# Two passes of 512-wide products for the last 1024 output columns of a hybrid encoder layer

## The chip, the cores and the metric

The kernel runs on one core of a Trainium2 chip. Its time is the device time of one execution in microseconds; where several executions were timed, the median is given. A profiled execution is a separate one, with a span (first to last instruction) of its own.

## What is computed

One layer of an encoder: 512 tokens of width 2048 are normalised and projected; eight attention heads and a bidirectional linear recurrence each make 1024 features per token; these 2048 mixed features are gated and projected back by `w_out`, and the residual `x` is added. The change concerns the last line alone.

```python
h = rms_norm(x, norm_w)
q, k, v, g_attn, xr, g_lru = split(h @ w_in)
...
mixed = concatenate([rms_norm(attn_out, attn_norm_w) * silu(g_attn),
                     rms_norm(lru_out, lru_norm_w) * silu(g_lru)], axis=-1)
return x + mixed @ w_out          # (512 x 2048) @ (2048 x 2048)
```

## The kernel before, in words

Everything is float32. A matrix product is made of three matmuls on numbers split in a high and a low part (high x high, high x low, low x high), each part in the type float32r. The split of a weight tile is a cast on ScalarE (the high part) and a subtraction on VectorE (the low part).

The stages run one behind the other on TensorE: the input projections (`proj_feat`, `proj_tok`, whose matmuls are on lines 145 to 147), recurrence, attention, gates, and then `outputs` (line 729). The order of TensorE's instructions is the program's own (`manual_schedule`, line 825). On the other engines a list scheduler orders them by priority; `tc.high_priority(AHEAD)` moves what prepares the weights 600 places ahead.

`outputs` works in four groups `c` of 512 output columns. Within a group the loop `i` runs over eight row pairs of `mixed`, that is 2 x 128 rows of `w_out`. `wraw` (line 189) loads a pair's 2 x 128 x 512 block of `w_out` (512 KB) on SyncE's queue, into one of three buffers.

The first six pairs are multiplied by a two-by-two block scheme with seven products instead of eight. The blocks on the weight side are 128 rows by 256 columns (`H`), those on the features' side 128 features by 256 tokens. `combine` (line 682) makes the block sums, `seven` (line 696) splits the three plain blocks and the four sums (768 + 1024 columns) into high and low parts, and `mult` (line 744) issues a product's matmuls, line 752: two blocks of 128 tokens, three terms, 256 columns each, 42 matmuls per pair. Four of the products (`P1`, `Q6`, `Q5`, `Q7`) go into shared sums in four PSUM banks of tag `pj`, the other three straight into the banks of their outputs, tag `mm`. Behind pair 5 the shared sums are combined (lines 805 to 812) into `comb` and added to `xt`, which holds `x`.

The last two pairs, 6 and 7, are split by `four` (line 704) and multiplied whole, by `whole` (line 762, matmuls on line 773): 24 matmuls of 512 columns per pair. In the last group one token block is done in halves of 256 columns, so that the final addition and store are short. At a group's end VectorE adds the banks to `xt` (line 818), and SyncE stores it (line 819).

The stationary side of these matmuls is the features' side, split and combined once and used by all four groups. `kept` (line 714) gives it its tiles, through `aside` (line 709), which makes a tile 16 floats longer and uses it from the eighth float on. The pairs 4 to 7 are prepared by `later` (line 965) and `last_gates` (line 985), a generator that `outputs` advances one step per pair in group 0. `wkept` (line 719) gives the moving side one of three sets of buffers in turn. `hring` and `aring` (lines 99 and 100) are rings that hold the recurrence's and the attention's outputs; an eight-float tile `pad` (line 102) is allocated behind them.

Of the kernel before, what the change touches and what calls it, by code (L numbers as in the profile page):

```python
# [16 lines left out]
P = 128  # L17
SEQ = 512
# [37 lines left out]
def hybrid_kernel(  # L56
# [69 lines left out]
    def ev():  # L126

        for pool, n in (("lru", 4), ("qkv", 8), ("fin", 4)):
            if pool in pools:
                return pools[pool].tile([P, SEQ], F32, tag="ev", bufs=n, name=nm("ev"))  # L130
# [58 lines left out]
    def wraw(w, r0, c0, nk=1, queue=nc.sync):  # L189

        raw = pools["wr"].tile([P, 2, SEQ], F32, tag="wr", bufs=3, name=nm("wr"))
# [486 lines left out]

    def halves(t):
# [49 lines left out]
    def outputs(work):  # L729

        for c in range(DM // SEQ):
            xt, comb = (
                pools["out"].tile([P, NT, SEQ], F32, tag=t, bufs=1, name=nm(t)) for t in ("xt", "cb")
            )
            cs = slice(c * SEQ, (c + 1) * SEQ)
            rows_ = [slice(t * P, (t + 1) * P) for t in range(NT)]
            for t in range(NT):
                nc.sync.dma_start(xt[:, t], xf[rows_[t], cs])

            acc = {k: pj().rearrange("p (s e) -> p s e", e=H) for k in (P1, Q6, Q5, Q7)}  # L740
            own = [mm() for _ in range(NT)]
            fresh = set(acc) | set(range(NT))

            def mult(k, s, ah, al, a, bh, bl, b_, last):
                ts_ = slice(s * P, (s + 1) * P)
                if k in acc:
                    dst, bank = acc[k][:, s, :], k
                else:
                    bank = s if k == Q4 else 2 + s
                    dst = own[bank][:, H:] if k in (P2, Q4) else own[bank][:, :H]  # L750
                for lh, rh in ((ah, bh), (ah, bl), (al, bh)):
                    nc.tensor.matmul(  # L752
                        dst, lh[:, a, ts_], rh[:, b_, :], start=bank in fresh,
                        stop=last and s == 1 and rh is bh and lh is al, skip_group_check=True,
                    )
                    fresh.discard(bank)


            end = c == DM // SEQ - 1
            lasts = [pj()[:, :H], own[1][:, H:]] if end else []  # L760

            def whole(t, ah, al, bh, bl, last):

                ts_ = slice(t % 2 * P, (t % 2 + 1) * P)
                for half in range(2 if t == 1 and end else 1):
                    for k in range(2):
                        a, w = 2 * k + t // 2, slice(2 * k, 2 * k + 2)
                        dst = own[t].rearrange("p (j e) -> p j e", e=H)
                        if t == 1 and end:
                            dst, w = lasts[half], 2 * k + half  # L770
                        for j, (lh, rh) in enumerate(((ah, bh), (ah, bl), (al, bh))):
                            new = t == 1 and end and half == 0 and k == 0 and j == 0 and not last
                            nc.tensor.matmul(  # L773
                                dst, lh[:, a, ts_], rh[:, w], start=new,
                                stop=last and k == 1 and j == 2, skip_group_check=True,
                            )

            for i, (r0, A) in enumerate(mixed):
                with tc.high_priority(AHEAD):
                    (raw,) = wraw(w_out, r0, c * SEQ)  # L780
                    if i < 6:
                        bh, bl = wkept(7)
                        seven(raw, ALU.add, bh, bl)
                    else:
                        bh, bl = wkept(4)
                        four(raw, bh, bl)
                if c == 0:
                    next(work, None)
                    A = mixed[i][1]
                ah, al = A  # L790
                if i < 6:
                    for k in (P1, Q6, Q5, Q7, P2, Q3, Q4):
                        for s in range(2):
                            mult(k, s, ah, al, k[0], bh, bl, k[1], i == 5 and k in (P1, Q6, Q5, Q7))
                else:
                    for t in (2, 3, 0, 1):
                        whole(t, ah, al, bh, bl, i == 7)
                if i == 5:
# [244 lines left out]
```

## Time and profile before

| | us |
|---|---|
| median of 3 runs (lowest, highest) | 665.76 (665.64, 665.89) |
| the profiled execution | 667.75 |
| its span | 666.0 |
| output groups in the span, from and to | 497.7 to 662.3 |

The views read here are the page (busy time of each engine, the chain of work that ended last, groups of instructions by line), the windows (busy time in stretches of the span), the timeline and the DMA issues. PE is TensorE's matmuls, PEld its weight loads, which overlap the matmuls, DVE VectorE, ACT ScalarE, POOL GpSimd, SP SyncE. Matmuls are pipelined: a row's mean ns is the time from a matmul's start to its end, and the next one starts before that. What a matmul costs in a stream is therefore read from a stretch of the chain divided by the number of matmuls in it.

### The profile page before, as it was taken

The page shows a single profiled execution, that of the slowest core. Times are in us where ns is not written, and L with a number is a line of the kernel's source. Part 1 is how long each engine was busy: PE and PEld are TensorE (multiplying, and loading weights), DVE is VectorE, ACT ScalarE, POOL GpSimd, SP SyncE. Part 2 cuts the span into 40 slices and gives each one's busy share as a digit, 9 for nine tenths or more (in the row PEclk, how much of TensorE's full clock was granted, in tenths as well). Part 3 has the DMA queues.
Part 4 walks back from the last instruction along what each step waited for, and adds up shares of the span by engine and source line. Part 5 has one row for each costly group of instructions (what it writes and reads, how often), then busy time and mean ns, then how long its engine had stood idle before and what let it go on. Part 6 is the DMA issues. An engine that isn't in the chain of part 4 may idle for free.

```text
span 666.0 us, 9502 instructions
## 1 busy us (share of the span) xinstructions
PE 660.9 (99%) x3599; PEld 570.4 (86%) x3599; DVE 488.8 (73%) x820; ACT 330.4 (50%) x580; POOL 58.8 (9%) x79
## 2 busy tenths in 40 slices
PE   9999999999999999999999999999999999999997
PEld 7888888888888888888888888888889999899996
DVE  4878788977688864656955577449989994967944
ACT  3533798589766416444734465345435333332320
POOL 0000000000022303011222212110000000000000
PEclk9999999999999999999999999999999999999999
DMA  8843252322334312322111221223335373462711
GB/s 287 284 118 105 64 165 65 95 63 75 85 126 127 101 57 63 95 64 63 53 44 63 64 64 36 68 87 95 94 105 181 113 216 115 141 197 76 252 32 63
DMA packets 43773, 71.06 MB, mean 107 GB/s; under 512 B 2776, under 2 KB 13136, under 8 KB 43728
## 3 DMA queue, kind: packets, MB, share of 16 engines
q1 hardware_dynamic: 43408, 69.93, 34.3%
q10 hardware_dynamic: 320, 0.53, 0.3%
q8 instruction: 28, 0.46, 0.3%
q14 instruction: 17, 0.14, 0.1%
HBM read 66.25 MB, written 4.19 MB: 106 GB/s over the span
## 4 chain that ended last, share of the span: by engine, by line
PE 97%; DVE 1%; DMA 1%; issue 0%; ACT 0%; ACTq 0%; DVEq 0%
PE pj L145 19%; PE pj L147 19%; PE pj L146 19%; PE pj L752 10%; PE mm L752 8%; PE mm L773 6%; PE mm L145 3%; PE mm L147 3%; PE mm L146 3%; PE mm L592 2%; PE pj L298 1%; PE mm L232 1%; DMA wr<-in_w_in_dram 1%; PE mm L535 1%; DVE k L412 0%; DVE wl L207 0%
## 5 line engine op out<-in xcount | busy, mean ns | idle before, releaser
L145 PE MATMUL pj<-x,wh 128*128 128x512 f32 x376 | 149.2, 397 | 0.0
L147 PE MATMUL pj<-x,wl 128*128 128x512 f32 x376 | 147.0, 391 | 0.0
L146 PE MATMUL pj<-x,wh 128*128 128x512 f32 x376 | 146.4, 389 | 0.0
L207 DVE TENSOR_TENSOR wl<-wr,wh 128x512 fp32r<-128x512 f32 x144 | 100.8, 722 | 29.7 <-ACT wh L206 29.6
L206 ACT CAST wh<-wr 128x512 fp32r<-128x512 f32 x143 | 85.6, 618 | 68.6 <-PE pj L147 25.7
L147 PEld LDWEIGHTS pj<-x,wl 128*128 128x128 f32 x376 | 70.6, 188 | 15.3
L145 PEld LDWEIGHTS pj<-x,wh 128*128 128x128 f32 x376 | 70.6, 188 | 13.7 <-DVE ev L377 0.5
L146 PEld LDWEIGHTS pj<-x,wh 128*128 128x128 f32 x376 | 70.7, 188 | 13.4
L145 PE MATMUL pj<-wh,x 128*128 128x512 f32 x192 | 74.9, 390 | 0.0
L147 PE MATMUL pj<-wh,x 128*128 128x512 f32 x192 | 74.8, 389 | 0.0
L146 PE MATMUL pj<-wl,x 128*128 128x512 f32 x192 | 74.7, 389 | 0.0
L752 PE MATMUL pj<-wl,mh 128*128 128x256 f32 x192 | 54.0, 281 | 0.0
L752 PE MATMUL pj<-wh,ml 128*128 128x256 f32 x192 | 54.0, 281 | 0.0
L752 PE MATMUL pj<-wh,mh 128*128 128x256 f32 x192 | 53.9, 281 | 0.0
L701 ACT CAST wh<-wr 128x768 fp32r<-128x768 f32 x24 | 20.1, 836 | 63.6 <-issue 47.1
L594 ACT CAST b<-mm 128x512 fp32r<-128x512 f32 x32 | 18.7, 586 | 61.5 <-PE mm L592 61.5
L580 DVE TENSOR_REDUCE mx<-mm 128x1 f32<-128x512 f32 x32 | 22.0, 688 | 33.0 <-PE mm L147 32.4
L146 PEld LDWEIGHTS pj<-wl,x 128*128 128x128 f32 x192 | 36.0, 188 | 7.5
L145 PEld LDWEIGHTS pj<-wh,x 128*128 128x128 f32 x192 | 36.0, 188 | 7.5
L147 PEld LDWEIGHTS pj<-wh,x 128*128 128x128 f32 x192 | 36.0, 188 | 7.5
L752 PE MATMUL mm<-wl,mh 128*128 128x256 f32 x144 | 40.5, 281 | 0.0
L752 PE MATMUL mm<-wh,ml 128*128 128x256 f32 x144 | 40.5, 281 | 0.0
(216 smaller groups left out, 1335.5 us busy)
## 6 DMA issues: line engine op xcount, KB each, us to landing
wr<-in_w_in_dram SPq DMA_DIRECT2D x71, 512.0 KB, 3.7
wr<-in_w_out_dram SPq DMA_DIRECT2D x32, 512.0 KB, 4.0
xt<-in_x_dram SPq DMA_DIRECT2D x16, 256.0 KB, 4.6
out_dram<-xt SPq DMA_DIRECT2D x15, 256.0 KB, 3.6
b<-in_x_dram SPq DMA_DIRECT2D x7, 512.0 KB, 9.2
k<-in_lru_wa_dram SPq DMA_DIRECT2D x8, 128.0 KB, 3.7
k<-in_lru_wx_dram SPq DMA_DIRECT2D x8, 128.0 KB, 3.3
b<-in_x_dram SPq DMA_DIRECT2D x2, 256.0 KB, 5.3
```

What stands on the lines that cost most here:

```text
L145: nc.tensor.matmul(acc, lh, rh, start=start, stop=False)
L146: nc.tensor.matmul(acc, lh, rl, start=False, stop=False)
L147: nc.tensor.matmul(acc, ll, rh, start=False, stop=stop)
L206: copy(hi, raw[:, k, :])
L207: nc.vector.tensor_sub(lo, raw[:, k, :], f(hi))
L232: nc.tensor.transpose(pt[:, t * P : (t + 1) * P], xc[:, t, ks], ident)
L580: nc.vector.tensor_reduce(mx, sc, axis=AX.X, op=ALU.max, negate=True)
L592: nc.tensor.transpose(pt[:, s * P : (s + 1) * P], p[:, s * P : (s + 1) * P], ident)
L594: nc.scalar.copy(pth[:, :, tt], p3)
L701: nc.scalar.copy(hi[:, to], part)
L752: nc.tensor.matmul(dst, lh[:, a, ts_], rh[:, b_, :], start=bank in fresh, stop=last and s == 1 and rh is bh and lh is al, skip_group_check ...
L773: nc.tensor.matmul(dst, lh[:, a, ts_], rh[:, w], start=new, stop=last and k == 1 and j == 2, skip_group_check=True,)
```

## The change

The groups 0 and 1 stay as they were, without the special last group. The groups 2 and 3 become one group of 1024 columns, `outputs_wide`. Its blocks are 512 columns wide, and all eight pairs go by seven products. Three of the products run in a first pass over the eight pairs, four in a second, since each product's sum now takes two banks and eight are there.

- First pass: each pair's `w_out` block is read without its last quarter, two block sums are added in place, three blocks are split. The three sums (`P1`, `Q6`, `Q5`) are combined at the end of the pass into `xs`; `x` is added to `xs` by eight accumulating DMAs that GpSimd's queue issues, in place of eight loads on SyncE's.
- Second pass: each pair's block is read again, whole; two plain blocks and two sums are split, in two sets of the weight buffers. In pair 7 the order of the two sets is turned round. At the end VectorE adds or subtracts the four sums (`Q7`, `Q4`, `Q3`, `P2`) into `xs`, and SyncE stores 128 x 512 pieces, the last of them in halves.
- The raw blocks lie in the space of `aring` (two) and in that of the weight ring (one).
- Since pairs 6 and 7 now need the block sums of the features' side too, `last_sums` makes them during group 1.
- `kept` no longer goes through `aside`, and `pad` is allocated ahead of the rings instead of behind them. `wraw` takes its buffers from a ring of the same size.

```diff
-    opened("wr", "left")
+    wring = opened("wr", "left").ring(3 * 4096, name="wring")
...
+    opened("pad", "right").tile([P, 8], F32, name="pad")
     hring = opened("hq", "right").ring(8 * 2048, name="hring")
     aring = pools["hq"].ring(8 * 2048, name="aring")
-    opened("pad", "right").tile([P, 8], F32, name="pad")
...
     def kept(pool, n=7):
-        return [
-            aside(lambda *a: pool.tile(*a, tag=t, bufs=1, name=t), n)
-            for t in (nm("mh"), nm("ml"))
-        ]
+        return [pool.tile([P, n, H], F32R, tag=t, bufs=1, name=t) for t in (nm("mh"), nm("ml"))]
...
+        rings = [aring, aring, wring]
+        def raw_blocks(i, n, turn):
+            raw = rings[turn % 3].tile([P, 4, SEQ], F32, name=nm("wr"))
+            r0 = mixed[i][0]
+            for k in range(2):
+                w = slice(cs[0].start, cs[0].start + min(2, n - 2 * k) * SEQ)
+                nc.sync.dma_start(
+                    raw[:, 2 * k : min(n, 2 * k + 2)].rearrange("p j e -> p (j e)"),
+                    w_out[r0 + k * P : r0 + (k + 1) * P, w],
+                )
+            return raw
+        def parts(blocks, n):
+            hi, lo = (t.rearrange("p n e -> p (n e)") for t in wkept(7))
+            hi, lo = (t[:, : n * SEQ].rearrange("p (n e) -> p n e", e=SEQ) for t in (hi, lo))
+            nc.scalar.copy(hi, blocks)
+            nc.vector.tensor_sub(lo, blocks, f(hi))
+            return hi, lo
+        def product(k, dst, i, b, n):
+            ah, al = part(i, k[0])
+            bh, bl = (t[:, n] for t in b)
+            for s in range(2):
+                ts_ = slice(s * P, (s + 1) * P)
+                for j, (lh, rh) in enumerate(((ah, bh), (ah, bl), (al, bh))):
+                    nc.tensor.matmul(
+                        dst[s], lh[:, ts_], rh, start=i == 0 and j == 0, stop=i == 7 and j == 2
+                    )
+        p1, q6, q5 = [pj(), pj()], [pj(), pj()], [mm(), mm()]
+        for i in range(8):
+            with tc.high_priority(AHEAD):
+                raw = raw_blocks(i, 3, i)
+                nc.vector.tensor_add(raw[:, 0], raw[:, 0], raw[:, 1])
+                nc.vector.tensor_add(raw[:, 2], raw[:, 2], raw[:, 0])
+                b = parts(raw[:, 0:3], 3)
+            for k, dst, n in ((P1, p1, 1), (Q6, q6, 2), (Q5, q5, 0)):
+                product(k, dst, i, b, n)
+        with tc.high_priority(AHEAD):
+            for s in range(2):
+                nc.scalar.copy(xs[1][:, 2 + s], p1[s])
+            for s in range(2):
+                nc.vector.tensor_sub(xs[1][:, s], xs[1][:, 2 + s], q6[s])
+            for s in range(2):
+                nc.vector.tensor_sub(xs[0][:, 2 + s], q5[s], xs[1][:, s])
+                nc.scalar.copy(xs[0][:, s], xs[0][:, 2 + s])
+            for t in range(NT):
+                for j in (0, 1):
+                    nc.gpsimd.dma_start(xs[j][:, t], xf[tokens[t], cs[j]], accum_op=ALU.add)
+        q3, p2, q7, q4 = [mm(), mm()], [pj(), pj()], [pj(), pj()], [mm(), mm()]
+        for i in range(8):
+            with tc.high_priority(AHEAD):
+                raw = raw_blocks(i, 4, 8 + i)
+                bs = [((Q3, q3, 0), (P2, p2, 1), parts(raw[:, 2:4], 2))]
+                nc.vector.tensor_add(raw[:, 0:2], raw[:, 0:2], raw[:, 2:4])
+                nc.vector.tensor_add(raw[:, 1], raw[:, 1], raw[:, 0])
+                bs.append(((Q7, q7, 0), (Q4, q4, 1), parts(raw[:, 0:2], 2)))
+            for *ks, b in bs[::-1] if i == 7 else bs:
+                for k, dst, n in ks:
+                    product(k, dst, i, b, n)
+        with tc.high_priority(AHEAD):
+            def add(t, j, acc, op=ALU.add, leave=True, cut=1):
+                for m in range(cut):
+                    e = slice(m * SEQ // cut, (m + 1) * SEQ // cut)
+                    nc.vector.tensor_tensor(xs[j][:, t, e], xs[j][:, t, e], acc[:, e], op=op)
+                    if leave:
+                        to = slice(cs[j].start + e.start, cs[j].start + e.stop)
+                        nc.sync.dma_start(of[tokens[t], to], xs[j][:, t, e])
+            for s in range(2):
+                add(s, 0, q7[s])
+                add(s, 1, q7[s], ALU.subtract, False)
+            for s in range(2):
+                add(s, 1, q4[s])
+            for s in range(2):
+                add(2 + s, 0, q3[s])
+            for s in range(2):
+                add(2 + s, 1, p2[s], cut=1 + s)
...
+    def last_sums():
...
+        for i, (hi, lo) in zip((6, 7), places):
+            for _ in range(2):
+                yield
+            sums_of[i] = [[t[n // 2][:, n % 2] for n in range(4)] for t in (hi, lo)]
+            res = combine(halves(ap_[i - 4]), ALU.subtract)
+            for n in range(2):
+                src = res[:, 2 * n : 2 * n + 2]
+                nc.scalar.copy(hi[n], src)
+                nc.vector.tensor_sub(lo[n], src, f(hi[n]))
-    outputs(last_gates())
+    outputs(0, last_gates())
+    outputs(1, last_sums())
+    outputs_wide(2)
```

More of the change, by code (lines that the diff above doesn't have):

```diff
@@ L727, in wkept @@
         ]
[L729 to L736, printed above, removed]
-            for t in range(NT):
[L738 to L798, printed above, removed]
-                    with tc.high_priority(AHEAD):
-                        def blk(i, j):
-                            return comb[:, 2 * i : 2 * i + 2, j * H : (j + 1) * H]
-                        v2 = fin_s((P, 2, H))
-                        nc.scalar.copy(blk(1, 1), acc[P1])
-                        nc.vector.tensor_sub(v2, acc[Q6], blk(1, 1))
-                        nc.vector.tensor_add(blk(1, 0), acc[Q5], v2)
-                        nc.vector.tensor_add(blk(0, 0), acc[Q7], blk(1, 0))
-                        nc.vector.scalar_tensor_tensor(
-                            blk(0, 1), acc[Q7], -1.0, v2, op0=ALU.mult, op1=ALU.subtract
-                        )
-                        nc.vector.tensor_add(xt, xt, comb)
-            with tc.high_priority(AHEAD):
-                parts = [(t, 0, SEQ, own[t]) for t in (2, 3, 0, 1)]
-                if end:
-                    parts[3:] = [(1, j * H, (j + 1) * H, lasts[j]) for j in range(2)]
-                for t, e0, e1, src in parts:
-                    nc.vector.tensor_add(xt[:, t, e0:e1], src, xt[:, t, e0:e1])
-                    nc.sync.dma_start(
-                        of[rows_[t], cs.start + e0 : cs.start + e1], xt[:, t, e0:e1]
-                    )
```

96 lines of the change are left out of this document (92 added, 4 removed).

## The prediction, as it was made

> **What bounds the kernel now.** I read the page's parts 1 and 4 first. The second line is the chain of work that ended last, by engine.
>
> ```profile
> PE 660.9 (99%) x3599; PEld 570.4 (86%) x3599; DVE 488.8 (73%) x820; ACT 330.4 (50%) x580; POOL 58.8 (9%) x79
> PE 97%; DVE 1%; DMA 1%; issue 0%; ACT 0%; ACTq 0%; DVEq 0%
> ```
>
> The end is set by the matmul stream alone; the other engines matter only where they would make it wait. So the question is how many microseconds of matmul issue the change takes out, and whether the stream stays fed. Next the windows view, on a projection stage, the four output groups (the change replaces the third and the fourth), and the two kinds of stretch inside the third.
>
> ```profile
> 70.00:220.00 150.00, 150.00 (x663) 124.22 (x662) 122.98 (x178) 118.75 (x216) 11.54 (x15) 1.00 0.33 97
> 497.70:538.90 41.20, 41.20 (x302) 39.07 (x301) 40.07 (x56) 19.70 (x23) 0.00 (x0) 1.00 0.44 139
> 538.90:579.90 41.00, 41.00 (x302) 38.87 (x301) 30.50 (x43) 13.40 (x15) 0.00 (x0) 1.00 0.48 151
> 579.90:620.90 41.00, 41.00 (x302) 38.87 (x301) 30.41 (x42) 13.30 (x15) 0.00 (x0) 1.00 0.49 154
> 620.90:662.30 41.40, 41.39 (x313) 39.57 (x311) 23.78 (x30) 9.74 (x11) 0.00 (x0) 1.00 0.32 109
> 579.90:609.90 30.00, 30.00 (x254) 30.00 (x253) 19.54 (x28) 9.72 (x11) 0.00 (x0) 1.00 0.52 168
> 609.90:620.90 11.00, 11.00 (x49) 8.87 (x49) 10.86 (x15) 3.58 (x4) 0.00 (x0) 1.00 0.39 116
> ```
>
> The columns are the stretch, its length, then busy time of PE, PEld, DVE, ACT and POOL, the granted clock, the DMA share and GB/s. PE has no gap in any group. DVE is nearly full in the first group (40.07 of 41.2) and has 10 us or more to spare in each later one; ACT and DMA are under half. In the seven-product stretch (579.9 to 609.9) the weight loads are busy all 30.00 us; in the stretch of 512-wide matmuls behind it they are not (8.87 of 11.0). The chain in order of time gives the pace of each shape (start, length, what):
>
> ```profile
> 568.84 11.15 PE mm L773 x48
> 579.99 2.83 PE pj L752 x24
> 582.82 2.12 PE mm L752 x18
> 599.88 2.88 PE pj L752 x24
> 602.77 2.16 PE mm L752 x18
> 661.58 0.73 PE mm L773 x6
> ```
>
> A row pair by seven products costs 2.83 + 2.12 = 4.95 us for 42 matmuls of 256 columns, 118 ns each; a later one 2.88 + 2.16 = 5.04, 120 ns each. A pair computed whole costs 11.15 / 2 = 5.57 us for 24 matmuls of 512 columns, 232 ns each. The projection's 512-wide matmuls go faster: 150 us / about 661 (two of the 663 only touch the edges) is 227 ns.
>
> **The change, part by part.**
>
> *Matmuls of the last 1024 columns.* Before, from 579.99 to the end of the last piece at 661.58 + 0.73 = 662.31: 82.3 us, PE full. After: 8 pairs x 7 products x 2 token blocks x 3 terms = 336 matmuls, all 512 wide. Two savings are in this: two 256-wide matmuls (236 ns) become one 512-wide one, and the two pairs that were computed whole (8 block products) take seven. At 227 ns the 336 cost 76.3 us, at 232 they cost 78.0. So the term is -6.0 or -4.3 us. I take 227: the stationary tiles of the 232 ns matmuls are the ones that `kept` places through `aside`, eight floats in, the projection's are not placed so, and the change takes `aside` away from `kept` and puts the 32-byte pad elsewhere. That the placement is the cause of the 5 ns is my reading of the code; no row separates it, so 232 stays as the other end.
>
> The Trainium skill, page "TensorE: Matmul & The Clock Gate", section "Back-to-back issue gap", gives N / 2.4 + 2.5 ns for matmuls back to back: 109 ns at 256 and 216 at 512. By it widening saves almost nothing per column, and the term would be, as an estimate, 504 x 109.2 + 96 x 215.8 - 336 x 215.8 = -3.2 us. The trace has 118 and 227 to 232, so its fixed part per matmul is four times the page's, and the measured figures decide.
>
> *Groups one and two.* They keep 42 matmuls of 256 columns for six pairs and 24 of 512 for two, but their stationary tiles move too. If the 96 whole matmuls go from 232 to 227 ns that is -0.5 us; the other end is 0. For the 504 of 256 columns the present pairs lie between 4.95 and 5.04 us, so I take 0, with -0.5 us below. Above, the nearest rows of 512-wide matmuls on differently placed tiles are these (busy us, mean ns):
>
> ```profile
> L145 PE MATMUL mm<-kt,b 128*128 128x512 f32 x32 | 12.9, 404 | 0.0
> L147 PE MATMUL pj<-wh,x 128*128 128x512 f32 x192 | 74.8, 389 | 0.0
> ```
>
> 404 - 389 = 15 ns more for each; on 504 matmuls +7.6 us is the far end.
>
> *Splitting the weights.* Rows by form, mean ns:
>
> ```profile
> L702 DVE TENSOR_TENSOR wl<-t,wh 128x1024 fp32r<-128x1024 f32 x24 | 29.2, 1220 | 1.1 <-ACT wh L701 1.1
> L702 DVE TENSOR_TENSOR wl<-wr,wh 128x768 fp32r<-128x768 f32 x24 | 22.9, 953 | 12.5 <-ACT wh L701 12.3
> L701 ACT CAST wh<-t 128x1024 fp32r<-128x1024 f32 x24 | 25.0, 1047 | 9.5 <-DVE t L689 9.5
> L701 ACT CAST wh<-wr 128x768 fp32r<-128x768 f32 x24 | 20.1, 836 | 63.6 <-issue 47.1
> L687 DVE TENSOR_TENSOR t<-wr 128x512 f32<-128x512 f32 x24 | 16.4, 687 | 12.7 <-DMA wr<-in_w_out_dram 12.6
> L453 DVE TENSOR_TENSOR b<-b,b 128x1024 f32<-128x1024 f32 x8 | 9.6, 1213 | 0.0
> L818 DVE TENSOR_TENSOR xt<-mm,xt 128x512 f32<-128x512 f32 x15 | 10.0, 683 | 6.0 <-PE mm L773 6.0
> L812 DVE TENSOR_TENSOR xt<-xt,cb 128x2048 f32<-128x2048 f32 x4 | 9.2, 2289 | 0.1
> ```
>
> Pass one, per pair, on DVE: two 512-wide adds (2 x 0.687) and one subtraction of 1536 columns, 1.04 ns a column from the first two rows, so 1.22 + 0.53 = 1.75 us: 3.1 us beside 18 x 227 ns = 4.1 us of matmul. ACT: one cast of 1536, 0.82 ns a column, 1.5 us. Pass two: 1.21 + 0.69 + 2 x 1.22 = 4.3 us of DVE and 2.1 of ACT beside 24 x 227 = 5.45 us. Both engines fit. If DVE ran strictly in order and waited out each cast, pass one would take 4.6 us per pair, 0.5 too many; over eight pairs that is 4 us, and the three buffer sets hold two pairs (8 us) of lead. So 0, with the seams below as its price. Group two takes on `last_sums`: two times a combination (0.69 + 2 x 0.42), two casts and two subtractions of 512, about 5.8 us of DVE. Its 30.5 busy of 41.0 us holds that.
>
> *Loads.* Pass one reads three 256 KB blocks per pair in 4.1 us (192 GB/s), pass two four in 5.45 (192 GB/s). SP issues 32 loads in place of 16; raw loads wait for a ring slot, and behind them on SP stand stores and further loads that nothing needs soon. The busiest stretch of the present output part, and the landing times:
>
> ```profile
> 538.90:548.90 10.00, 10.00 (x86) 10.00 (x85) 9.50 (x16) 3.67 (x4) 0.00 (x0) 1.00 0.86 274
> wr<-in_w_out_dram SPq DMA_DIRECT2D x32, 512.0 KB, 4.0
> ```
>
> 274 GB/s at a share of 0.86 means 319 at a full share, so 192 fits, at 0.60. The first raw tiles lie in `aring`, whose head pairs are last read in `last_sums` halfway through group two; the 4 us of landing is covered.
>
> *Seams.* At the end of pass one ACT copies two banks and DVE subtracts four (0.68 each) before the new sums may take the banks. P1 and Q6 end 2.7 and 1.4 us before the pass does, and pass two starts in two free banks (Q3, 1.4 us), takes P1's next, and needs Q5's last of all, 4.1 us in. Covered on paper; DVE work queued behind these subtractions is pair two's splitting, with a pair of lead. I allow +0.5 us for all seams (0 to +2). The eight accumulating x loads sit on POOL, which is idle here (0.00 in the windows above), and are needed 40 us later.
>
> *Tail.* Now one 256-wide add follows the last matmul, and the last stores land:
>
> ```profile
> 662.33 0.42 DVE L818 TENSOR_TENSOR xt<-mm,xt 128x256 f32<-128x256 f32 x1 [0.29 <-PE mm L773]
> 663.00:664.00 1.00, 0.00 (x0) 0.00 (x0) 0.00 (x0) 0.00 (x0) 0.00 (x0) 1.00 0.93 304
> ```
>
> After, DVE has nine adds of 512 and two of 256 behind the last pair, and Q7's first block is ready 21 matmuls (4.8 us) before the last matmul ends, at E. From E - 4.8 the queue takes 9 x 0.683 + 2 x 0.42 = 7.0 us: done at E + 2.2, where it is now E + 0.44. That is +1.8 us. Stores of 2.1 MB must leave in the same 7 us, 300 GB/s, just the 304 of the last row, so +0.4 more. Tail +2.2 us (+1.5 to +3).
>
> **Sum.** -6.0 - 0.5 + 0 + 0 + 0.5 + 2.2 = -3.8 us. The profiled execution took 667.75 us around a span of 666.0; its span would become 662.2. The runs' median is 665.76, so the forecast is **662.0 us**, 0.57% faster. A difference of about 0.2% (1.3 us) is what a measurement of this kernel can tell from none.
>
> **The rivals.**
>
> *Pace.* The wide matmuls stay at 232 ns and so do the whole ones: -4.3 + 0.5 + 2.2 = -1.6, 664.2 us. For it: every 512-wide row with these tiles is at 232. Against: all other 512-wide stages are at 227. Chance 0.13.
>
> *Narrow matmuls slow down.* The 504 of groups one and two lose by their new placement. At 5 ns each +2.5 us: 664.5; from 7.5 ns (3.8 us / 504) the change is lost. For it: `aside` is used for just such tiles, and their weight loads are already busy all the time. Against: no row shows a slower 256-wide matmul. Chance 0.12.
>
> *Starved (slower than before).* The accumulating loads hold the DMA engines and pass two waits for weights. Its 8.4 MB of weights and 2.1 MB of x at 319 GB/s take 32.9 of 43.6 us, 10.7 spare; 2.1 MB plain is 6.6 us. Accumulation must read both sides, and no row shows one. It decides when it takes 2.6 times as long as a plain load; at four times pass two lacks 19.8 - 10.7 = 9.1 us, net +5.3, 671.1 us. For it: DMA is the only resource that the change loads far more (154 to over 190 GB/s). Against: the lead in the buffers. Chance 0.20. The Trainium skill, page "DMA: Bandwidth & Descriptors", section "Issuing engines are not separate DMA queues", says that transfers of all issuers run on the same 16 engines and interleave, which is this rival's premise; before has too few issues from another queue to test it.
>
> The forecast itself has 0.55. **Range** 660.0 to 668.0: below it lies a gain at 118 ns with no seam and a short tail, above it most of the starved case. Faster by over 0.2%: 0.55 + most of the pace case + a quarter of the narrow one = 0.67; within: 0.10; slower: 0.23.
>
> **What would show it.** Right: the chain gives 18 wide matmuls in 4.1 us and 24 in 5.45; 48 whole ones in 10.9; no PE gap at the pass seam; DVE ends about 2.2 us behind the last matmul. Wrong: pairs of group one above 5.04 us (narrow), wide matmuls at 232 (pace), PE waiting on DVE or DMA for weights in pass two with a DMA share near 0.9 (starved), or a tail over 3 us longer.

## The result and the profile after

The changed kernel took **670.62 us** (median of 5 runs, 668.22 to 671.05); the kernel before, on the same chip, 665.68 us (665.4 to 665.89). The ratio is 1.0067, with a 95% interval of 1.0049 to 1.0086: 0.67% slower, where 0.57% faster was forecast. The profiled execution took 671.05 us, with a span of 669.3.

The two profiled executions start their output part at different times (the first output matmul at 497.61 us before, at 495.72 after). In the other traces it lies at 495.2 to 495.6, with the old placement of the tiles (p2 below) and with the new one (p1, e1), and at 496.6 to 497.0 with a tile of 32 to 128 bytes added; and the profiled execution of before, 667.75, is itself 2 us above its median. So these 2 us are not the change's (they are there before 21 us of the trace), and the parts are compared from the first output matmul to the end of the span: 168.4 us before, 173.6 after, **+5.2 us**.

The page of the changed kernel, busy times and then the chain of work that ended last, by engine:

```profile
PE 654.9 (98%) x3323; PEld 554.2 (83%) x3323; DVE 497.5 (74%) x818; ACT 337.3 (50%) x582; POOL 66.1 (10%) x87
PE 84%; DVE 8%; DMA 6%; issue 1%; SPq 0%; ACT 0%; DVEq 0%; ACTq 0%
```

Before, 97% of the chain was PE. Now 8% of it is DVE and 6% DMA: the matmul stream waits for something. The windows view says where (stretch, length, busy time of PE, PEld, DVE, ACT and POOL, granted clock, DMA share, GB/s):

```profile
497.60:538.90 41.30, 40.80 (x297) 38.54 (x296) 41.20 (x58) 18.84 (x23) 0.00 (x0) 1.00 0.53 175
578.80:611.50 32.70, 32.70 (x146) 27.04 (x145) 22.10 (x23) 11.98 (x10) 0.00 (x0) 1.00 0.68 216
615.00:620.00 5.00, 5.00 (x23) 3.86 (x21) 2.64 (x5) 3.14 (x5) 2.27 (x3) 1.00 1.00 229
620.00:625.00 5.00, 2.74 (x12) 2.17 (x12) 5.00 (x5) 1.03 (x1) 2.56 (x3) 1.00 0.90 168
625.00:630.00 5.00, 5.00 (x23) 4.13 (x23) 0.21 (x1) 2.11 (x2) 0.86 (x2) 1.00 1.02 266
630.00:635.00 5.00, 1.75 (x8) 1.11 (x7) 3.30 (x4) 1.04 (x1) 0.87 (x1) 1.00 1.08 303
635.00:640.00 5.00, 5.00 (x17) 3.92 (x16) 3.90 (x5) 1.05 (x1) 0.00 (x0) 0.66 0.94 245
640.00:662.90 22.90, 22.90 (x102) 18.76 (x100) 16.68 (x19) 6.33 (x6) 0.00 (x0) 1.00 0.24 87
```

Pass one (second row) is full: 32.7 us for eight times 18 matmuls, 4.08 us a pair, as forecast. Pass two is not. PE is busy 2.74 of 5 us from 620 and 1.75 of 5 us from 630, and from 635 it has a mean granted clock of 0.66. In just these 25 us the DMA share is 0.90 to 1.08, so the 16 engines have no idle time left, and afterwards it is 0.24. POOL, which issues the accumulating loads, is busy in the rows from 615 to 635 and in neither row ahead of them. The first row, nearly all of it group one, is a smaller surprise: DVE is busy 41.20 of 41.30 us.

The chain of waits in order of time (start, length, what) shows what ends the longer stall (lines left out are marked by dots):

```profile
613.90 5.99 DMA wr<-in_w_out_dram
...
622.36 0.33 SPq L829
...
622.74 8.84 DMA wr<-in_w_out_dram
...
631.70 1.23 DVE wr L881
632.93 1.15 DVE wl L839
...
634.12 1.62 PE mm L848 x5
635.74 4.16 PE pj L848 x12
639.90 2.74 PE mm L848 x12
```

A block takes 5.99 us to land; only when it is split can SP issue the next one into its buffer, at 622.36, and that one lands 8.84 us after its start: a late block makes a later one late. DVE, which has waited for it, adds and splits it (2.4 us), and PE, idle since 630.7, starts at 634.1. The next 12 matmuls take 4.16 us, and the 12 behind them 2.74: half the clock for a while, then the full one. Added up from the starts of the matmuls in the trace and set against 227 ns each, pass two waits 2.4 us at 619.7 and 3.4 us at 630.5, loses 1.7 us at half clock, and some 0.3 in small waits, **7.9 us** in all.

The tail, the same windows and the DVE timeline of the changed kernel:

```profile
663.00:664.00 1.00, 0.09 (x1) 0.00 (x0) 1.00 (x3) 0.00 (x0) 0.00 (x0) 1.00 1.10 334
665.00:666.00 1.00, 0.00 (x0) 0.00 (x0) 0.00 (x0) 0.00 (x0) 0.00 (x0) 0.97 1.12 321
667.00:668.00 1.00, 0.00 (x0) 0.00 (x0) 0.00 (x0) 0.00 (x0) 0.00 (x0) 0.50 0.29 78
```
```profile
658.32 0.69 DVE L893 TENSOR_TENSOR xt<-xt,pj 128x512 f32<-128x512 f32 x1 [1.09 <-PE pj L848]
663.11 1.34 DVE L893 TENSOR_TENSOR cb<-cb,pj 128x512 f32<-128x512 f32 x3
```

The additions run from 658.32 to 664.45, 1.5 us behind the last matmul's end at 662.9; then the stores drain, at 321 to 334 GB/s up to 666 and more slowly up to 667.8. From the start of the last matmul to the end it is 6.6 us, and was 4.0: +2.6.

### The profile page after: what moved, and what is told of

Its sections match the earlier page's. It is cut to its first block, busy times and chain, and to the rows that moved or that the text cites. A ratio compares the mean times of both kernels' runs of the same rounds, so it can differ in the third digit from the quotient of the medians.

```text
span 669.3 us, 8999 instructions
## 1 busy us (share of the span) xinstructions
PE 654.9 (98%) x3323; PEld 554.2 (83%) x3323; DVE 497.5 (74%) x818; ACT 337.3 (50%) x582; POOL 66.1 (10%) x87
## 4 chain that ended last, share of the span: by engine, by line
PE 84%; DVE 8%; DMA 6%; issue 1%; SPq 0%; ACT 0%; DVEq 0%; ACTq 0%
PE pj L145 19%; PE pj L147 19%; PE pj L146 19%; DMA wr<-in_w_out_dram 5%; PE mm L145 3%; PE mm L147 3%; PE mm L146 3%; PE pj L749 3%; PE mm L749 2%; PE mm L592 2%; PE pj L848 2%; PE mm L762 2%; PE mm L848 2%; DVE wl L839 2%; DVE wl L704 1%
## 5 line engine op out<-in xcount | busy, mean ns | idle before, releaser
L838 ACT CAST wh<-wr 128x1024 fp32r<-128x1024 f32 (+1 forms) x24 | 28.6, 1196 | 58.1 <-PE mm L848 22.7
L839 DVE TENSOR_TENSOR wl<-wr,wh 128x1024 fp32r<-128x1024 f32 (+1 forms) x24 | 33.4, 1397 | 4.7 <-ACT wh L838 4.7
L585 POOL TENSOR_SCALAR k<-k,sm 128x512 f32<-128x512 f32 x32 | 24.1, 753 | 124.0 <-DVE sm L584 112.5
L595 DVE TENSOR_TENSOR b<-mm,b 128x512 fp32r<-128x512 f32 x32 | 22.1, 689 | 12.1 <-ACT b L594 12.1
L749 PE MATMUL pj<-wh,ml 128*128 128x256 f32 x96 | 27.2, 283 | 0.0
L749 PE MATMUL pj<-wl,mh 128*128 128x256 f32 x96 | 27.2, 283 | 0.0
```

Source lines behind the costliest of these rows:

```text
L585: nc.gpsimd.tensor_scalar(p, p, sm, 0.0, op0=ALU.mult, op1=ALU.add)
L595: nc.vector.tensor_sub(ptl[:, :, tt], p3, f(pth[:, :, tt]))
L749: nc.tensor.matmul(dst, lh[:, a, ts_], rh[:, b_, :], start=bank in fresh, stop=last and s == 1 and rh is bh and lh is al, skip_group_check ...
L838: nc.scalar.copy(hi, blocks)
L839: nc.vector.tensor_sub(lo, blocks, f(hi))
```

## The experiments

The theory after the result: the eight accumulating loads hold the DMA engines while pass two needs its weights (the rival *starved*). Against it: the seam itself (the subtractions that free the banks) delays DVE; three buffers for the raw blocks are too few (the *ring rival* of the expectations); the loads' traffic, accumulating or not, is too much anywhere in pass two; or the new placement of tiles slows the matmuls. All times are medians, each with its ratio to the kernel before on the same chip.

| kernel | us (lowest to highest) | ratio, 95% interval |
|---|---|---|
| changed kernel | 670.62 (668.22 to 671.05) | 1.0067 [1.0049, 1.0086] |
| e1_no_x | 662.92 (662.74 to 663.21) | 0.9961 [0.9946, 0.9976] |
| e2_plain_x | 664.89 (663.30 to 665.44) | 0.9990 [0.9980, 0.9999] |
| e3_late_x | 665.52 (664.87 to 666.07) | 0.9998 [0.9988, 1.0008] |
| e4_spread_x | 667.01 (666.34 to 669.65) | 1.0028 [1.0019, 1.0037] |
| p1_before_placed | 665.65 (665.37 to 665.89) | 1.0003 [0.9994, 1.0012] |
| p2_no_x_old_place | 664.19 (663.71 to 664.62) | 0.9981 [0.9972, 0.9990] |
| f1_late_x64 | 664.69 (664.39 to 665.12) | 0.9988 [0.9979, 0.9996] |
| f2_late_x_tail | 664.55 (663.91 to 665.46) | 0.9988 [0.9979, 0.9997] |
| g1_late_x128 | 665.39 (665.26 to 665.73) | 0.9998 [0.9989, 1.0007] |
| g2_late_x_offset | 664.74 (664.44 to 665.24) | 0.9987 [0.9979, 0.9996] |
| e5_half_stores | 662.12 (662.00 to 662.25) | 0.9948 [0.9930, 0.9966] |
| h1_late_x256 | 663.08 (662.38 to 663.96) | 0.9966 [0.9953, 0.9978] |
| h2_late_x256_offset | 662.59 (661.92 to 663.09) | 0.9956 [0.9943, 0.9970] |
| h3_late_x_tail_offset | 663.33 (662.57 to 663.77) | 0.9966 [0.9953, 0.9978] |

**The loads left out.**

```diff
-            for t in range(NT):
-                for j in (0, 1):
-                    nc.gpsimd.dma_start(xs[j][:, t], xf[tokens[t], cs[j]], accum_op=ALU.add)
```

> The changed kernel without its eight accumulating loads: x is left out of the last 1024 output columns. Theory (the accumulating loads hold the DMA engines and the weights of pass two come late): both PE stalls of the changed kernel (2.4 and 3.4 us behind the pass seam) and the half-clock stretch after the second are gone, 8.4 us in all, so about 662 us, 0.5% under before. Rival (three raw tiles are too few, the loads come late by the ring alone): the stalls stay, shorter at most, and the time stays above 667 us.

662.92 us, 7.7 less than the changed kernel. Its two passes in the windows view:

```profile
578.50:611.10 32.60, 32.60 (x145) 26.98 (x144) 23.97 (x25) 11.98 (x10) 0.00 (x0) 1.00 0.66 217
611.10:654.70 43.60, 43.60 (x193) 35.86 (x192) 33.34 (x38) 15.88 (x16) 0.00 (x0) 1.00 0.40 138
```

Pass two is full, at the full clock. All seam work but the loads is still there, and so are the three buffers, so neither costs anything here by itself. The 336 wide matmuls take 578.45 to 654.49 + 0.23, 76.3 us, the forecast's number.

**The same bytes, plain** (the loads overwrite the sums).

```diff
-                    nc.gpsimd.dma_start(xs[j][:, t], xf[tokens[t], cs[j]], accum_op=ALU.add)
+                    nc.gpsimd.dma_start(xs[j][:, t], xf[tokens[t], cs[j]])
```

> The same eight loads from the same queue at the same place, but as plain copies that overwrite what pass one has left there, so the last 1024 columns lack the first pass's sums. If the bytes of the burst alone do the harm (2.1 MB ahead of the weights), the time stays near 670 us. If it is the accumulation (its packets hold the engines about 1.8 times as long as plain ones by the queue's share), the stalls shrink to under half: 663 to 666 us. By the ring rival: 667 us or more, no different from the run without x.

664.89 us. PE still waits 1.6 us at 619.1 and 0.9 at 629.0, with no half-clock stretch. The DMA view from 606 to 637 us (queue: packets, MB, share of the 16 engines; then issues, KB each, median us to landing), of the changed kernel, of the one without the loads, and of this one:

```profile
q0 software_dynamic: 1146, 2.09, 37.9%
wr<-in_w_out_dram SPq DMA_DIRECT2D x10, 512.0 KB, 5.9
cb<-in_x_dram POOLq DMA_DIRECT2D x4, 256.0 KB, 7.8
```
```profile
wr<-in_w_out_dram SPq DMA_DIRECT2D x10, 512.0 KB, 3.7
```
```profile
q0 software_dynamic: 640, 2.10, 17.6%
wr<-in_w_out_dram SPq DMA_DIRECT2D x10, 512.0 KB, 4.6
cb<-in_x_dram POOLq DMA_DIRECT2D x4, 256.0 KB, 6.2
```

For the same 2.1 MB the accumulating loads hold the engines for 37.9% of 31 us, 11.7 us, and the plain ones for 17.6%, 5.5 us: **2.15 times**. The accumulating loads travel in packets half as large: in the trace 1024 packets of 2 KB, 182 ns each, against 512 of 4 KB, 169 ns each (the counts in the view include 128 packets of 4 bytes). The weights land in 5.9 us beside the accumulating loads, 4.6 beside the plain ones and 3.7 without any. So the traffic alone, at this moment, costs about a quarter of the loss (664.89 - 662.92 = 2.0 of 7.7 us), and accumulation the rest.

Why a plain load still costs 2 us, the chains show. The third block of pass two is issued just behind the seam; in e2_plain_x, and in h1_late_x256 (below), where no load of `x` runs before 637 us, it lands like this (start, length; in this order):

```profile
612.35 6.02 DMA wr<-in_w_out_dram
```
```profile
612.43 4.72 DMA wr<-in_w_out_dram
```

With 4.72 us PE already waits 0.3 us for this block, at 619.2; with 6.02 it waits 1.6. There is hardly any lead at the seam (in e1_no_x the block is issued 1.0 us earlier and PE does not wait), so what the block loses to other traffic goes into PE's wait. In the changed kernel it took 5.99 us and PE waited 2.4. About 1 us of this is not the loads' doing: reckoned from the first output matmul, the block was issued 1 us later than in h1_late_x256 (613.90 and 612.43), before the first load of `x` was issued at 614.43.

**The same loads, later.** In these two GpSimd copies one column of a raw block into a marker tile, and the loads are issued behind that copy: all eight when pair seven's weights of pass two are there (`i == 6`), or one per pair.

```diff
+                if i == 6:
+                    mark = nc.gpsimd.tensor_copy(const([P, 1], "mark"), raw[:, 3, 0:1])
+                    with tc.issue_after(mark.ins):
+                        for t in range(NT):
+                            for j in (0, 1):
+                                nc.gpsimd.dma_start(
+                                    xs[j][:, t], xf[tokens[t], cs[j]], accum_op=ALU.add
+                                )
```

> All eight accumulating loads are held back until the weights of pair 6 of pass two have landed, when only one weight load is still to come. Theory: no PE stall at the seam, 662 to 663 us, unless the additions at the very end now wait for x (then the tail grows by 1 to 3 us). Ring rival: still above 667 us.

> One accumulating load for each pair of pass two, issued when that pair's weights have landed; three of them come together at the seam because three pairs are loaded ahead. Theory: a third of the burst at a time, so stalls under 2 us in all, 662 to 664 us. Ring rival: above 667 us.

Both miss what was expected of them. e3_late_x has no stall, yet takes 665.52 us. e4_spread_x is worse, 667.01: a block issued at 619.5, beside a load of `x`, takes 8.0 us to land, PE waits 2.5 us for it at 627.3, and the clock falls. Rows of e4_spread_x and of the changed kernel:

```profile
629.00:630.00 1.00, 0.00 (x0) 0.00 (x0) 1.00 (x2) 0.00 (x0) 0.00 (x0) 1.00 0.49 82
631.00:632.00 1.00, 1.00 (x4) 0.78 (x3) 1.00 (x2) 0.00 (x0) 0.45 (x1) 0.50 0.21 35
```
```profile
636.00:637.00 1.00, 1.00 (x4) 0.81 (x3) 0.14 (x1) 0.00 (x0) 0.00 (x0) 0.50 0.77 152
639.00:640.00 1.00, 1.00 (x6) 0.78 (x6) 1.00 (x2) 0.43 (x1) 0.00 (x0) 1.00 1.02 320
```

Why e3_late_x was no faster was the next question. Its wide matmuls ran at 231 ns in place of 227, which is 1.5 us over 336. Either the loads beside them cost that, or the marker tile does, since it shifts every address behind it. The wide matmuls of e4_spread_x, with loads beside them too, stay at 227 ns where the clock is full; in the built programs its eight markers take 8 x 32 = 256 bytes, the one of e3_late_x 32.

**The placement.** Two kernels exchange the placement alone: p1 is the kernel before with the changed kernel's (no `aside`, `pad` ahead of the rings), p2 is e1_no_x with the old one.

```diff
+    opened("pad", "right").tile([P, 8], F32, name="pad")
     hring = opened("hq", "right").ring(8 * 2048, name="hring")
     aring = pools["hq"].ring(8 * 2048, name="aring")
-    opened("pad", "right").tile([P, 8], F32, name="pad")
...
+        return [pool.tile([P, n, H], F32R, tag=t, bufs=1, name=t) for t in (nm("mh"), nm("ml"))]
```

> The kernel before with the placement alone of the change: kept without aside, pad ahead of the rings. Theory (where the stationary tile starts against the moving one sets the pace): the whole matmuls go from 232 to 227 ns (-0.9 us over some 180), and every seven-product pair takes 5.04 us in place of 4.97 on the mean (+1.7 us over 24 pairs), together +0.8 us, a tenth of a per cent. Rival (the placement does nothing, the paces of the changed kernel come from its tile shapes): both paces stay as they were, no difference.

> The changed kernel without the accumulating loads (x left out of the last 1024 columns) and with the placement of before: kept through aside, pad behind the rings. Theory: the wide matmuls run at 232 ns in place of 227, so the 336 take 78.0 us in place of 76.3 (a seventh of them, on the sums of pairs 6 and 7, stay at 227, so some 77.7), the pairs of the first two groups go back to 4.97; against the run without x and with the new placement the time is 0.8 to 1.2 us longer. Rival: no difference from that run.

The chain in order of time, of p1, of p2, and of h1 (below):

```profile
566.86 10.91 PE mm L769 x48
577.77 2.87 PE pj L748 x24
580.64 2.16 PE mm L748 x18
```
```profile
560.00 2.13 PE mm L752 x18
567.09 11.15 PE mm L765 x48
578.24 2.79 PE pj L851 x12
```
```profile
567.58 10.91 PE mm L762 x48
578.48 2.72 PE pj L848 x12
```

With the new placement 48 whole matmuls take 10.91 us (227 ns) and 18 narrow ones 2.16 (120.0); with the old 11.15 (232) and 2.13 (118). In p1 the narrow ones lose some 1.1 us and the whole ones gain some 0.9: no difference in time that can be measured, where +0.8 us was expected. In p2 the wide matmuls are at 232, and it takes 1.3 us more than e1_no_x. So the placement is the cause of the 5 ns, and it costs 1 to 2 ns on the narrow ones.

What about the placement decides? I took the start addresses of every matmul's moving tile and of the stationary tile loaded for the next matmul from the built programs, and set their distance against the intervals in all sixteen traces, from the first output matmul on (waits and the half clock left out). At a distance of a multiple of 256 bytes a 512-wide matmul takes 227.7 ns on the mean (4433 of them); at every other distance 230 to 233 (1870). For 256-wide ones it is the other way round: 119.9 at multiples (5038), 117 to 120 elsewhere, 118 on the mean (4042). The rule is not whole. In g2_late_x_offset (below) about half of the wide distances are multiples, and these 201 matmuls take 230.8 ns like their neighbours; in p2 the 40 at multiples take 231.3. So 227 ns is shown for streams in which nearly all distances are multiples. This rule was found in steps: the next three runs were made before it was whole. A marker of 64 or 128 bytes was to bring the 227 ns back.

```diff
-                    mark = nc.gpsimd.tensor_copy(const([P, 1], "mark"), raw[:, 3, 0:1])
+                    mark = nc.gpsimd.tensor_copy(const([P, 16], "mark")[:, :1], raw[:, 3, 0:1])
```

> The late accumulating loads again, but the marker tile that holds them back is 64 bytes in place of 4, so that it does not move the weight tiles behind it by 32 bytes. Placement theory: the wide matmuls go back from 231 to 227 ns, 1.6 us less than the first late run, about 663.9 us, 0.25% under before. Rival (the late loads themselves slow the matmuls through the memory): the pace stays at 231 ns and the time at 665.5.

> The accumulating loads held back until pair 6 of pass two, with a marker tile of 128 bytes, so that moving and stationary tiles again start a multiple of 128 bytes apart as in the changed kernel. Theory (the pace hangs on that distance modulo 128 bytes): all 336 wide matmuls at 227 ns, 76.1 us from the first to the last, about 663.2 us, 0.35% under before. Rival (the late loads slow the matmuls): 229 to 233 ns as in the two runs with smaller markers, 664.7.

It did not: 229 to 233 ns at 64 bytes and 231 at 128 (77.2 and 77.4 us for the 336), 664.69 and 665.39 us. g2 took g1 and put the moving tiles of the twelve narrow pairs 64 bytes further, in tiles 128 bytes larger:

```diff
-                    bh, bl = wkept(7)
+                    bh, bl = wkept(7, 16)
```

> As the last, and the moving tiles of the seven-product pairs in the first two groups start 64 bytes further, the others not. Theory: those 504 matmuls go from 120 to 118 ns (-1.1 us), the 512-wide ones stay at 227: about 662.1 us, the fastest of all here, 0.5% under before. Rival: the pace of the 256-wide ones does not hang on the distance, no difference from the last.

The narrow matmuls did go to 117.6 ns, the wide ones stayed at 231: 664.74 us.

**A marker of 256 bytes.** It moves every address behind it by 256 bytes, so the distances stay what they were, counted modulo 256.

```diff
-                    mark = nc.gpsimd.tensor_copy(const([P, 32], "mark")[:, :1], raw[:, 3, 0:1])
+                    mark = nc.gpsimd.tensor_copy(const([P, 64], "mark")[:, :1], raw[:, 3, 0:1])
```

> f1_late_x64 with a marker tile of 256 bytes in place of 64, so that every start address behind it moves by 256 bytes and each distance from a matmul's moving tile to the next stationary tile stays as in the changed kernel (0 by 256 for 423 of the 432 wide and whole matmuls and for all 504 narrow ones). Theory (the accumulating loads cost what they take from the weights in flight, and the loss that stayed in the late versions is the marker's shift): no TensorE wait over 0.5 us in the wide part, wide matmuls at 227 ns again, first to last wide matmul 76.0 to 76.3 us as without the loads, tail 6.4 to 6.6 us, median 662.8 to 663.4 us. Rival (late accumulating loads themselves slow the matmuls, whatever the placement): wide stays at 231 ns, 77.2 to 77.6 us, median 664.2 to 665.4 us.

663.08 us. Pass two of this kernel:

```profile
611.00:654.90 43.90, 43.80 (x193) 35.78 (x191) 34.07 (x38) 15.89 (x16) 7.33 (x9) 1.00 0.70 184
```

The wide matmuls are back at 227 ns (2.72 us for 12 in the rows above) beside accumulating loads in the same pass. From the first to the last wide matmul it is 76.5 us, where e1_no_x has 76.0; 0.3 of the difference is the wait at 619.2, long before the loads. So late loads do not slow matmuls, the marker did. It did so in the earlier stages too: of the 1.9 us between the spans of f1_late_x64 and this kernel (663.2 and 661.3), 1.4 lie ahead of the first output matmul (496.6 and 495.2). Moved to where the weights no longer need the engines, the eight loads cost 0.2 us in the medians (663.08 - 662.92), within the spread of the runs, where they cost 7.7 behind the seam.

h2 adds the 64-byte offset of the narrow moving tiles, in tiles 256 bytes larger.

> h1_late_x256 with the moving tiles of the twelve narrow pairs put 64 bytes further in tiles 256 bytes larger, so that the narrow distance is 192 and no other distance changes. Theory (the distance decides the pace): narrow 117.6 ns as in g2_late_x_offset against 120.0, 504 x 2.4 = 1.2 us less than h1_late_x256, wide still 227 ns, median 661.6 to 662.2 us. Rival (the faster narrow matmuls came in g2_late_x_offset with slower wide ones and one cannot be had without the other): the same time as h1_late_x256 within 0.4 us.

662.59 us, between the two expectations. The narrow matmuls went to 117.8 ns, 1.1 us over 504, but 0.4 of it went into a longer wait in group one (1.0 us at pair eight in place of 0.65). It has the lowest median of the complete versions, 0.44% under before, but its runs overlap with those of h1_late_x256.

**The tail.**

```diff
+                bs = []
+                if i < 6:
+                    bs.append(((Q3, q3, 0), (P2, p2, 1), parts(raw[:, 2:4], 2)))
+                else:
+                    held.append((i, raw))
...
+        for i, raw in held:
+            with tc.high_priority(AHEAD):
+                b = parts(raw[:, 2:4], 2)
+            for k, dst, n in ((Q3, q3, 0), (P2, p2, 1)):
+                product(k, dst, i, b, n)
```

f2 is f1 with this order and the loads one pair earlier: in the last two pairs Q7 and Q4 come first, Q3 and P2 of both last. h3 is h2 with the same. e5 is e1_no_x with half of the stores sent at the seam.

> As the last, with the loads of x held back until pair 5 of pass two, and the last two pairs turned round: first the products Q7 and Q4 of pairs 6 and 7, then Q3 and P2 of both, so that six of VectorE's last additions and four of the last stores fall beside 24 matmuls. Theory (the tail is longer by the queue of last additions and stores): the span behind the last matmul's start shrinks from 6.5 to about 4.5 us, 661.5 to 662.5 us. Rival (the tail's length comes from the end of the program, not from the stores): still 6.5 us, 664.

> h2_late_x256_offset with the order of f2_late_x_tail: the loads behind pair six, and in the last two pairs Q7 and Q4 of both before Q3 and P2 of both, so that half of the final additions and stores start 5 us before the last matmul. Theory: tail 5.7 us in place of 6.5, 0.5 us of TensorE wait in the middle of pass two as in f2_late_x_tail, so 0.2 to 0.8 us less than h2_late_x256_offset: 661.0 to 661.8 us. Rival (earlier accumulating loads collide with the last weights): no gain, 661.8 to 662.6 us.

> The changed kernel without the accumulating loads, and with half of the last 2.1 MB stored at the seam, before the values are finished (x is left out, and the first of the two column halves holds only the first pass's sums). VectorE's additions at the end stay. Theory (the tail is as long as its stores take, some 300 GB/s): the time from the last matmul's start to the end of the span falls from 6.5 to about 4.5 us. Rival (VectorE's queue of additions sets it): it stays above 6 us.

The tail (last matmul's start to the end) fell from 6.5 to 5.8 us in both f2 and h3, where f2 had been expected at 4.5. But the wide part is 0.5 us longer in f2 (than in f1) and 0.9 in h3 (than in h2), most of it a wait in the middle of pass two, on the weights' splitting again. The waits of h3:

```profile
DVE wr L892 <- DMA wr<-in_w_out_dram: 12.9, 6, 2.8
PE pj L850 <- DVE wl L841: 0.7, 1, 0.7
```

f2 at 664.55 us is level with f1. h3 at 663.33 us has a median 0.7 above h2's (the runs overlap), outside both its expectations: loads one pair earlier collide with the last weights, as its rival had it, and cost more than the rival allowed. In e5 the tail is 5.4 us, between its theory and its rival, so the volume of the last stores is worth about 1 us of the 6.5. Its windows:

```profile
657.00:658.00 1.00, 0.00 (x0) 0.00 (x0) 0.00 (x0) 0.00 (x0) 0.00 (x0) 1.00 1.01 362
658.00:659.00 1.00, 0.00 (x0) 0.00 (x0) 0.00 (x0) 0.00 (x0) 0.00 (x0) 1.00 0.50 147
```

Even the last half of the stores leaves in a burst behind the additions, and 1.7 us pass between its last packet (658.7) and the end (660.4).

**The wait in group one** needed no run of its own. Waits of the changed kernel in 530 to 533 us, then the DVE rows of p1 and of e1_no_x that make the last feature tile:

```profile
PE mm L762 <- DVE ml L709: 0.5, 1, 0.5
```
```profile
521.55 1.23 DVE L706 TENSOR_TENSOR ml<-av,mh 128x1024 fp32r<-128x1024 f32 x1 [0.78 <-ACT mh L705]
```
```profile
530.92 1.22 DVE L709 TENSOR_TENSOR ml<-av,mh 128x1024 fp32r<-128x1024 f32 x1
```

The subtraction is 9 us later than in p1, and the matmuls that want it wait for it (from 531.5 to 532.2 in e1_no_x). What is new on DVE in group one, by line and form, in e1_no_x:

```profile
L693 DVE TENSOR_TENSOR t<-av 128x512 f32<-128x512 f32 x1 | 0.7, 689 | 0.0
L858 DVE TENSOR_TENSOR wr<-wr 128x512 f32<-128x512 f32 x1 | 0.7, 687 | 0.0
L857 DVE TENSOR_TENSOR wr<-wr 128x512 f32<-128x512 f32 x1 | 0.7, 684 | 0.0
```

The scheduler pulled the first wide block's two additions and a piece of `last_sums` ahead into group one, 2.1 us on an engine that had 1.1 to spare. That these made the subtraction late is read from the rows and was not tried by itself.

## Why the prediction was wrong

Term by term, from the traces, in us from the first output matmul to the end:

| step | forecast | measured |
|---|---|---|
| wide matmuls for the last 1024 columns | -6.0 | -6.0 (e1_no_x: 76.3 for 82.3) |
| groups one and two | -0.5 | +0.8 |
| seams and loads | +0.5 | +7.9 |
| tail | +2.2 | +2.6 |
| sum | -3.8 | +5.3 (the whole: +5.2) |

- **Loads and seams: the step that failed.** The prediction put the accumulating loads at nothing because they are needed 40 us later and POOL is idle. When they are needed says nothing of whom they hold up: they start at once, behind the seam. The rival *starved* named this and was given 0.20. Its mechanism came true; its threshold did not. It set the spare DMA time of the whole pass, 10.7 of 43.6 us, against the accumulation and had it decide at 2.6 times the plain load. Measured were 2.15 times its plain form (11.7 us), or 1.8 times the 6.6 us that the prediction reckoned, under the threshold, and still 7.9 us were lost. That its price, 671.1 us at four times, lies near the measured 670.62 is luck. The average over the pass hides where the transfers run: 25 us from 615 to 640 at a share near 1.0, with 0.24 behind them, where the spare time lay. In these 25 us the pass needs 3.3 us of DMA per 5.45 us of matmul, 15 us, for its weights, and `x` took 11.7: 26.7 in 25.
- **The lead, beside the sum.** A sum that fits is not enough either: with the plain loads it is 15 and 5.5 in 25, and PE still waited 2.4 us. The prediction counted on the buffers' lead and had pass two covered at the seam; the third block of pass two comes with hardly any (in h1_late_x256 PE waits 0.3 us for it though no load of `x` is near), so it lands late by what other traffic takes, and each late block held back the issue of a later one (the chain above).
- The Trainium skill, page "DMA: Bandwidth & Descriptors", section "Issuing engines are not separate DMA queues", has all issuers' transfers interleave on the same 16 engines. By that rule weights land later whenever POOL's loads run, and the traces agree: 3.7 us without them, 5.9 with them.
- **Wide matmuls: right**, to 0.1 us, and the reading that placement makes the 5 ns is now shown by p1 and p2. The rule of 256 bytes, as far as it goes, the prediction did not have.
- **Groups one and two.** Whole matmuls gained 0.3 (228.7 ns for 232.2), where 0.5 was forecast. Narrow ones were put at 0 and lost 0.5 (504 at 120.0 for 118.9): the rival *narrow* at a fifth of its price. The remaining 0.65 is the wait at pair eight, and its likely cause, not tried by itself, is this: `last_sums` was placed in group two, where DVE has room, but work with high priority is also pulled ahead into group one, where it has not.
- **Tail: right in kind, 0.4 short.** The additions end at E + 1.5, not 2.2; the stores take longer behind them (last packet at 667.8, 3.4 us after the last addition; before, 1.5).
- Without the failed step (e1_no_x, 662.92 us) the kernel is 0.9 us above the forecast; by its trace that is +1.3 from the groups, +0.3 from the tail and -0.5 from the seam, which costs nothing there.
- One reading beside the sum is off. By the prediction's own figures 118, 227 and 232 ns leave 11, 14 and 19 ns over N / 2.4, which is 4.5 to 7.5 times the formula's 2.5. The Trainium skill, page "TensorE: Matmul & The Clock Gate", section "Back-to-back issue gap", calls the formula the gap of an isolated matmul and gives about 131 ns for a stream at 512 columns; no stream here comes near that, the fastest being at 227. Nothing hangs on either.

What stays open: why the blocks of pass one came later in the profiled execution of the changed kernel, which gave 1 us of its first wait; what an issue that comes earlier at the seam, or a fourth buffer, would save, which no run tried; what mechanism stands behind the 256 bytes, and why the rule fails in g2_late_x_offset.

## What to carry to other kernels

A transfer that is needed late is not free because of it: ask when it starts, add up the DMA time over that stretch and not over the stage, and ask how much lead each load beside it has there. Without lead, a load that lands 1.3 us later costs 1.3 us even where the sum fits. Loads that nobody waits for belong behind the last load that somebody waits for; here that was worth 7.5 us and took one marker. A marker or pad of a few bytes moves every address behind it, so in a kernel like this give such tiles 256 bytes before reading anything from a difference of 0.2%.

## What the runs showed of the hardware

- The distance between the start of a matmul's moving tile and that of the next stationary tile goes with the pace: 227 ns at multiples of 256 bytes and 230 to 233 elsewhere (512 wide), but 119.9 against 118 on the mean (256 wide). In g2_late_x_offset, where only about half are multiples, these take 230.8 too.
- Accumulating loads from DRAM into SBUF hold the DMA engines 2.15 times as long as plain loads of the same bytes on the same queue (11.7 and 5.5 us for 2.1 MB), in packets of 2 KB in place of 4. In the later kernels it was 11.9 to 13.2 us.
- Behind PE waits of 3.41 us (the changed kernel) and 2.53 us (e4_spread_x) the granted clock stands at 0.50 for 3.41 us, starting some 1 us after the matmuls resume, and the matmuls start 427 ns apart; behind a wait of 2.42 us (the changed kernel, 619.7) it stays at 1.00. The length of the wait does not decide alone. In every trace the changes of the clock lie whole multiples of 3.41 us apart; in the changed kernel they come at 635.23, 638.64 and 665.95 us. If windows are drawn on that grid, the clock fell at the end of a window with 2.3 us of idle PE (the changed kernel) and of one with 2.5 us (e4_spread_x), while the wait at 619.7 lies across a border, at 621.58, with 1.6 us in one window and 0.8 in the next. So the limit lies between 1.6 and 2.3 us of idle time in one such window; these few cases are all that the runs show. The Trainium skill, page "TensorE: Matmul & The Clock Gate", section "What's actually happening", gives half rate after at least one idle window of about 3.4 us, the windows running free of the work. The grid agrees; but neither window was idle throughout, so here the measurement decides.
